# Routing stage of an expert layer: which engine subtracts the low halves of the weight stream

## The chip, the cores and the metric

The kernel runs on one core of one Trainium2 chip. The metric is the device time of one execution in microseconds (us). In the kernel before, three executions took 1796.3 us in the median (1794.24 to 1799.25).

Five engines work side by side, each through its own list of instructions in order: TensorE (PE, matrix products; PEld is its weight load), VectorE (DVE), ScalarE (ACT), GpSimd (POOL), and SyncE (SP), which here only issues loads. An instruction waits until the semaphores that it names have been raised by other engines or by DMAs.

## What is computed

Two transformer blocks in a row, on 256 positions of width 1024. The change lies in the last layer of the second block, a product-key layer with 16384 one-neuron experts. Cut to that layer, the reference is:

```
q = (x @ wq).reshape(B, L, 8, 2, 128)
s = jnp.einsum('blhpd,hpkd->blhpk', q, keys)            # 128 keys in each of 16 lists
ts, ti = lax.top_k(s, 16)                               # 16 best of each list
cand = ts[..., 0, :, None] + ts[..., 1, None, :]        # 16 x 16 sums for each head
cs, ci = lax.top_k(cand.reshape(B, L, 8, 256), 16)
e1 = take_along_axis(ti[..., 0, :], ci // 16, axis=-1)
e2 = take_along_axis(ti[..., 1, :], ci % 16, axis=-1)
g = softmax(cs)
act = gelu(x_t . u_tab[e]) * g                          # for each of the 8 x 16 chosen experts
out = sum of act * v_tab[e]
```

The kernel computes the product of x with the whole of `u_tab` (128 blocks of 128 experts), spreads the chosen weights into a dense matrix, and multiplies with the whole of `v_tab`. So which experts are chosen is needed only when the dense matrix is built.

## The kernel before

**The weight stream.** All weights come as 544 blocks of 128 x 1024 in the order of use. SP loads each block into one of three `raw` buffers. Products are computed from rounded operands in three matmuls each, so each block is split: ACT copies `raw` to a rounded high half `wh` (line 250), and the low half `wl` is `raw` minus `wh` (line 252), made by VectorE or by GpSimd. There are four buffers each of `wh` and `wl`. `Stream.next()` hands out block i and first writes the split of block i + 3 into the instruction lists. A `raw` buffer can be loaded again once its low half is made. The rule for the engine is one attribute, `pool_every`: 0 gives every low half to VectorE, 1 every one to GpSimd, and 2 those of even number.

**The products.** `gemm_w` takes one block as eight groups of three matmuls: high half by the high x (line 304), high half by the low x (305), low half by the high x (306).

**The queries.** Sixteen blocks of `wq` give sixteen query tiles `qb` (line 1437). For each, two steps later, four short matmuls with `keys` (1421), and one step after that two searches `top16` on VectorE (lines 1411 to 1415), each of five operations over 128 scores: eight largest, their positions, replacement, again eight largest and positions.

**The routes.** Beside the first blocks of `u_tab` (`experts_in`: two blocks, one gelu on ACT at line 1396, one store of the result) runs the generator `route`, once for each half of the positions. Each block is followed by one step of it. The 18 steps of one route are: one with the cast `vf` and the 128 x 2048 sum `cand`; eight with a search of 256 candidates each; one with the softmax (`ex`, an Exp on ACT at line 1460, `pos`, `ee`); six wide ones of 128 x 2048 elements that look the indices up (twice a comparison at 1475, a product at 1478, a reduction at 1480); one empty one; one with three transposes on PE (1485), which read the reductions' result; and one with their copy `eT`, in which the next route begins. The two routes go with 20 pairs of blocks. After them, with `pool_every` at 0, the remaining 88 blocks of `u_tab` go side by side with the dense matrix, most of whose work is VectorE's (lines 1518 to 1539).

**What sets the order.** Every engine's list is written out by the program's order; nothing is rearranged afterwards. A low half that VectorE makes stands in its list between the pieces of searches and routes; one that GpSimd makes stands in a list that holds nothing else in this stage.

Of the kernel before, what the change touches and what calls it, by code (L numbers as in the profile page):

```python
# [283 lines left out]
def body(ctx, tc, a, o, upto=99):  # L284
# [4 lines left out]
    ws = Stream(nc, P0, [a["ws"], a["us"], a["vs"]])  # L289
    pump = Pump()  # L290

    def psum(tag):
        return PS.tile([128, 512], F32, tag=tag, name=tag, bufs={"mm": 2, "acc": 3, "od": 1, "tr": 2}[tag])
# [14 lines left out]
    def gemm_w(out, w, xs, nk=8, base=0):  # L308
        h, lo = w
        for n in range(nk):  # L310
            sl = slice((base + n) * 128, (base + n + 1) * 128)
            mm3(out, h[:, sl], lo[:, sl], xs[0][n], xs[1][n], n == 0, n == nk - 1)

    def gemm_pair(outs, xs, shared=False):

        ws_ = [ws.next(), ws.next(AHEAD - 1)]
        for low in range(2):
            for n, k in enumerate(KORD):
                sl = slice(k * 128, k * 128 + 128)
                for i in range(2):  # L320
                    h, lo = ws_[i]
                    if low:
                        nc.tensor.matmul(outs[i], lo[:, sl], xs[0][k], start=False,
                                         stop=n == 7 and not (shared and i == 0))
                    else:
                        nc.tensor.matmul(outs[i], h[:, sl], xs[0][k], start=n == 0 and not (shared and i), stop=False)
                        nc.tensor.matmul(outs[i], h[:, sl], xs[1][k], start=False, stop=False)
# [1061 lines left out]
    def experts_in(i, between=pump.step):  # L1389
        pt = psum("mm")  # L1390
        gemm_w(pt[:, :T], ws.next(), xs_x)
        between()
        gemm_w(pt[:, T:], ws.next(), xs_x)
        st = PP.tile([128, 2, T], F32, tag="st", name="st", bufs=2)
        last[i] = st
        nc.scalar.activation(st, pt.rearrange("p (e t) -> p e t", e=2), AF.Gelu_apprx_tanh)  # L1396
        if i < 62:
            nc.scalar.dma_start(stored[i // 4][:, 2 * (i % 4):2 * (i % 4) + 2, :], st)
# [3 lines left out]
    with tc.tile_pool(name="route", bufs=1) as RP:  # L1402
        keys = RP.tile([128, 16, 128], F32, name="keys")
        nc.gpsimd.dma_start(keys, a["keys"])
        nc.gpsimd.dma_start(iota, a["iota"])
        v = RP.tile([128, 2, 16, 16], F32, name="v")
        vi = RP.tile([128, 2, 16, 16], U32, name="vi")

        def top16(val, idx, src, n):
            scr = RP.tile([128, 256], F32, tag="scr", name="scr", bufs=1)  # L1410
            nc.vector.max(val[:, 0:8], src)
            nc.vector.max_index(idx[:, 0:8], val[:, 0:8], src)
            nc.vector.match_replace(scr[:, :n], val[:, 0:8], src, -3.0e38)
            nc.vector.max(val[:, 8:16], scr[:, :n])
            nc.vector.max_index(idx[:, 8:16], val[:, 8:16], scr[:, :n])

        def key_scores(b, qb):
            yield
            pt = psum("acc")
            for tt in range(2):  # L1420
                nc.tensor.matmul(pt[:, tt * 128:tt * 128 + 128], qb[:, tt * 128:tt * 128 + 128], keys[:, b, :],
                                 start=True, stop=True)
            yield
            for tt in range(2):
                top16(v[:, tt, b], vi[:, tt, b], pt[:, tt * 128:tt * 128 + 128], 128)

        first = [psum("mm"), psum("mm")]
        gemm_pair([pt[:, :T] for pt in first], xs_x)
        for b in range(16):
            if b < 2:  # L1430
                pt = first[b]
            else:
                pt = psum("mm")
                ws.pool_every = 2
                gemm_w(pt[:, :T], ws.next(), xs_x)
            qb = RP.tile([128, T], F32, tag="qb", name="qb", bufs=3)
            nc.scalar.copy(qb, pt[:, :T])
            pump.step()
            pump.add(key_scores(b, qb))

        def route(tt):
            B4 = [128, 8, 16, 16]
            vf = RP.tile([128, 16, 16], F32, tag="vf", name="vf", bufs=1)
            nc.vector.tensor_copy(vf, vi[:, tt])
            cand = RP.tile([128, 8, 256], F32, tag="cand", name="cand")
            vv = v[:, tt].rearrange("p (h two) k -> p h two k", two=2)
            fv = vf.rearrange("p (h two) k -> p h two k", two=2)
            nc.vector.tensor_tensor(cand.rearrange("p h (i j) -> p h i j", i=16),
                                    vv[:, :, 0, :, None].to_broadcast(B4),
                                    vv[:, :, 1, None, :].to_broadcast(B4), op=ALU.add)  # L1450
            cs = RP.tile([128, 8, 16], F32, tag="cs", name="cs", bufs=1)
            ci = RP.tile([128, 8, 16], U32, tag="ci", name="ci", bufs=1)
            yield
            for h in range(8):
                top16(cs[:, h], ci[:, h], cand[:, h], 256)
                yield
            ee = RP.tile([128, 3, 8, 16], F32, tag="ee", name="ee", bufs=1)
            ex = RP.tile([128, 8, 16], F32, tag="ex", name="ex", bufs=1)
            nc.vector.tensor_tensor(ex, cs, cs[:, :, 0:1].to_broadcast([128, 8, 16]), op=ALU.subtract)
            nc.scalar.activation(ex, ex, AF.Exp)  # L1460
            pos = RP.tile([128, 2, 8, 16], F32, tag="pos", name="pos", bufs=1)
            cf = RP.tile([128, 8, 16], F32, tag="cf", name="cf", bufs=1)
            nc.vector.tensor_copy(cf, ci)
            nc.vector.tensor_scalar(pos[:, 0], cf, 1.0 / 16.0, -7.5 / 16.0, op0=ALU.mult, op1=ALU.add)
            nc.vector.tensor_scalar(pos[:, 0], pos[:, 0], MAGIC, None, op0=ALU.add)
            nc.vector.tensor_scalar(pos[:, 0], pos[:, 0], -MAGIC, None, op0=ALU.add)
            nc.vector.scalar_tensor_tensor(pos[:, 1], pos[:, 0], -16.0, cf, op0=ALU.mult, op1=ALU.add)
            sm = RP.tile([128, 8], F32, tag="sm", name="sm", bufs=1)
            nc.vector.tensor_reduce(sm, ex, axis=AX.X, op=ALU.add)
            nc.vector.reciprocal(sm, sm)  # L1470
            nc.vector.tensor_tensor(ee[:, 2], ex, sm[:, :, None].to_broadcast([128, 8, 16]), op=ALU.mult)
            yield
            for p in range(2):
                oh = RP.tile([128, 8, 16, 16], F32, tag="oh", name="oh")
                nc.vector.tensor_tensor(oh, pos[:, p, :, :, None].to_broadcast(B4),
                                        iota[:, None, None, :16].to_broadcast(B4), op=ALU.is_equal)
                yield
                nc.vector.tensor_tensor(oh, oh, fv[:, :, p, None, :].to_broadcast(B4), op=ALU.mult)
                yield
                nc.vector.tensor_reduce(ee[:, p], oh, axis=AX.X, op=ALU.add)  # L1480
                yield
            yield
            pt = psum("tr")
            for n in range(3):
                nc.tensor.transpose(pt[:, n * 128:n * 128 + 128], ee[:, n].rearrange("p h k -> p (h k)"), ident)
            yield
            nc.scalar.copy(eT[tt], pt[:, :384].rearrange("p (n t) -> p n t", n=3))

        def route_all():
            yield  # L1490
            yield
            for tt in range(2):
                yield from route(tt)

        pump.add(route_all())
        while pump.active:
            experts_in(n_in[0])
            n_in[0] += 1
            pump.step()
        ws.pool_every = 0  # L1500
# [135 lines left out]
```

## Time and profile before

| what | before |
|---|---|
| median of three executions | 1796.3 us |
| the profiled execution | 1792.96 us |
| its span, first to last instruction | 1791.1 us |
| PE busy, share of the span | 97% |
| DVE busy | 74% |
| ACT busy | 52% |
| POOL busy | 18% |
| mean granted clock of TensorE | 0.991 |
| granted clock, 950 to 1146 us | 0.97 |

The queries begin at about 950 us of the span, the first block of `u_tab` at about 1000, the first matmuls of the dense matrix at 1146.5. A busy share is a mean over stages with different limits; what matters for this change is what PE waits for between 950 and 1146. In a row of the timeline the first number is the start, the second the duration, both in us; a bracket at the end gives how long the engine had been idle before it and what ended that. PEclk is the granted clock of TensorE as a share of full speed: 1.00 is 2.4 GHz, 0.50 is 1.2 GHz.

### The profile page before, as it was taken

The numbers are of one execution on the slowest core, as the hardware profiler recorded it, in microseconds if no ns is written. First come the engines' busy times: TensorE is split into PE (matmuls) and PEld (weight loads), VectorE is DVE, ScalarE is ACT, GpSimd is POOL, SyncE is SP. The second block draws the span as 40 slices with busy tenths as digits, with TensorE's granted clock in tenths as the row PEclk, the third lists the DMA queues.
The fourth block names the chain that finished last, engine by engine and source line by source line (L and its number), as shares of the span: only waits on it lengthen the run. The fifth ranks groups of instructions, "written<-read, shape, count | busy, mean of one in ns | idle before, by whom it ended". The sixth has DMA issues, their size and how long they took to land.

```text
span 1791.1 us, 30504 instructions
## 1 busy us (share of the span) xinstructions
PE 1729.7 (97%) x11790; PEld 1581.5 (88%) x11794; DVE 1332.6 (74%) x2177; ACT 936.1 (52%) x1515; POOL 319.1 (18%) x249
## 2 busy tenths in 40 slices
PE   8999999999999999999899889899999999999998
PEld 7999888999899987997799889899999988888886
DVE  5665668855665645888767999899999977776766
ACT  5544556545464435685545345455555545545554
POOL 3000133221300101000003344100000033333332
PEclk9999999999999999999999999999999999999999
DMA  7656453444476653553255456566665677777775
GB/s 235 191 174 196 148 164 106 138 134 156 162 216 190 198 166 117 167 188 106 91 180 191 140 189 219 199 195 190 200 198 191 199 249 252 243 241 240 244 239 173
DMA packets 93410, 332.08 MB, mean 185 GB/s; under 512 B 10552, under 2 KB 10707, under 8 KB 90960
## 3 DMA queue, kind: packets, MB, share of 16 engines
q1 hardware_dynamic: 79488, 287.73, 50.0%
q0 software_dynamic: 3696, 21.67, 3.6%
q10 hardware_dynamic: 10080, 20.71, 3.2%
q8 instruction: 93, 1.52, 0.4%
q14 instruction: 53, 0.43, 0.1%
HBM read 311.73 MB, written 18.35 MB: 184 GB/s over the span
## 4 chain that ended last, share of the span: by engine, by line
PE 62%; DVE 26%; issue 4%; ACT 4%; DMA 3%; POOL 1%; ACTq 0%; POOLq 0%; SPq 0%; DVEq 0%
PE mm L304 10%; PE mm L306 9%; PE mm L305 9%; PE acc L306 7%; PE acc L305 7%; PE acc L304 7%; DVE wl L252 7%; DVE oh L1523 5%; DVE gd L1539 2%; PE od L304 2%; PE od L305 2%; PE od L306 2%; DVE oh L1518 2%; ACT wh L250 2%; DMA raw<-in_us_dram 1%
## 5 line engine op out<-in xcount | busy, mean ns | idle before, releaser
L252 DVE TENSOR_TENSOR wl<-raw,wh 128x1024 fp32r<-128x1024 f32 x502 | 651.9, 1302 | 281.7 <-ACT wh L250 279.6
L306 PE MATMUL mm<-hT,wl 128*128 128x256 f32 (+1 forms) x2496 | 706.5, 283 | 10.7 <-DVE wl L252 10.7
L304 PE MATMUL mm<-hT,wh 128*128 128x256 f32 (+1 forms) x2496 | 715.0, 286 | 1.7 <-ACT rxp L1227 1.3
L250 ACT CAST wh<-raw 128x1024 fp32r<-128x1024 f32 x544 | 570.4, 1052 | 262.1 <-DMA raw<-in_us_dram 73.2
L305 PE MATMUL mm<-lT,wh 128*128 128x256 f32 (+1 forms) x2496 | 706.3, 283 | 0.0
L306 PEld LDWEIGHTS mm<-hT,wl 128*128 128x128 f32 x2496 | 475.5, 191 | 11.7 <-DVE wl L252 11.7
L304 PEld LDWEIGHTS mm<-hT,wh 128*128 128x128 f32 x2496 | 475.1, 190 | 10.4 <-issue 5.5
L305 PEld LDWEIGHTS mm<-lT,wh 128*128 128x128 f32 x2496 | 473.9, 190 | 3.4 <-issue 1.4
L306 PE MATMUL acc<-wh,al 128*128 128x512 f32 x516 | 202.1, 392 | 0.5 <-DVE al L344 0.5
L304 PE MATMUL acc<-wh,ah 128*128 128x512 f32 x516 | 202.0, 391 | 0.0
L305 PE MATMUL acc<-wl,ah 128*128 128x512 f32 x516 | 201.5, 391 | 0.1
L252 POOL TENSOR_TENSOR wl<-raw,wh 128x1024 fp32r<-128x1024 f32 x42 | 111.1, 2646 | 198.0 <-ACT wh L250 198.0
L1523 DVE SCALAR_TENSOR_TENSOR oh<-iota,eT,wp 128x256 fp32r<-128x256 f32 x256 | 117.3, 491 | 0.0
L306 PEld LDWEIGHTS acc<-wh,al 128*128 128x128 f32 x516 | 96.8, 188 | 21.8 <-DVE al L344 1.1
L305 PEld LDWEIGHTS acc<-wl,ah 128*128 128x128 f32 x516 | 96.9, 188 | 20.2 <-DVE wl L252 0.5
L304 PEld LDWEIGHTS acc<-wh,ah 128*128 128x128 f32 x516 | 96.9, 188 | 19.2 <-issue 0.3
L343 ACT CAST ah<-sv 128x256 fp32r<-128x256 f32 x124 | 50.5, 407 | 120.6 <-PE od L305 44.8
L344 DVE TENSOR_TENSOR al<-sv,ah 128x256 fp32r<-128x256 f32 x124 | 77.5, 625 | 39.0 <-ACT ah L343 38.8
L1564 POOL TENSOR_TENSOR sv<-sv,gd 128x512 f32<-128x512 f32 x62 | 101.3, 1660 | 5.7 <-DMA sv<-act 5.3
L1396 ACT ACTIVATE st<-mm 128x512 f32<-128x512 f32 x64 | 38.3, 598 | 75.9 <-PE mm L306 75.8
L1538 ACT COPY gd<-acc 128x256 f32<-128x256 f32 x128 | 46.5, 402 | 59.3 <-PE acc L1533 42.9
L417 POOL TENSOR_SCALAR ssq<-ssq 128x1 f32<-128x1 f32 x18 | 8.1, 450 | 356.4 <-ACT junk L415 327.6
(388 smaller groups left out, 2198.5 us busy)
## 6 DMA issues: line engine op xcount, KB each, us to landing
raw<-in_ws_dram SPq DMA_DIRECT2D x288, 512.0 KB, 3.8
raw<-in_us_dram SPq DMA_DIRECT2D x128, 512.0 KB, 3.6
raw<-in_vs_dram SPq DMA_DIRECT2D x128, 512.0 KB, 4.3
act<-st ACTq DMA_DIRECT2D x62, 256.0 KB, 2.7
sv<-act POOLq DMA_DIRECT2D x15, 1024.0 KB, 7.7
gate_w<-in_gate_w_dram ACTq DMA_DIRECT2D x2, 1024.0 KB, 5.6
gain<-in_gains_dram POOLq DMA_DIRECT2D x3, 512.0 KB, 6.7
res<-x SPq DMA_DIRECT2D x2, 512.0 KB, 4.2
```

Source lines behind the costliest of these rows:

```text
L250: nc.scalar.copy(h, raw)
L252: eng.tensor_tensor(lo, raw, h.bitcast(F32), op=ALU.subtract)
L304: nc.tensor.matmul(out, lh, rh, start=start, stop=False)
L305: nc.tensor.matmul(out, lh, rl, start=False, stop=False)
L306: nc.tensor.matmul(out, ll, rh, start=False, stop=stop)
L343: nc.scalar.copy(h, src)
L344: (eng or nc.vector).tensor_tensor(lo, src, h.bitcast(F32), op=ALU.subtract)
L1396: nc.scalar.activation(st, pt.rearrange("p (e t) -> p e t", e=2), AF.Gelu_apprx_tanh)
L1518: nc.vector.tensor_tensor(o1, iota[:, None, :].to_broadcast([128, ONE, 128]), eT[tt][:, 0, tl:tl + ONE, None].to_broadcast([128, ONE, 128] ...
L1523: nc.vector.scalar_tensor_tensor(oh, iota[:, None, :].to_broadcast([128, 2, 128]), eT[tt][:, 1, tl:tl + 1], wp[:, :, tl:tl + 1].bitcast(F3 ...
L1538: nc.scalar.copy(g, v[:, 1])
L1564: nc.gpsimd.tensor_tensor(src, src, gd[:, e:e + 2, :], op=ALU.mult)
```

## The change

Four assignments of `pool_every`. In the queries, from the third block on, it becomes 1 instead of 2. In a route it becomes 0 before `cand`, 1 before the eight searches, and 0 again before the softmax. The old value held from the queries to the end of the routes.

```
@@ queries
                 pt = psum("mm")
-                ws.pool_every = 2
+                ws.pool_every = 1
                 gemm_w(pt[:, :T], ws.next(), xs_x)
@@ route
             nc.vector.tensor_copy(vf, vi[:, tt])
+            ws.pool_every = 0
             cand = RP.tile([128, 8, 256], F32, tag="cand", name="cand")
...
             yield
+            ws.pool_every = 1
             for h in range(8):
                 top16(cs[:, h], ci[:, h], cand[:, h], 256)
                 yield
+            ws.pool_every = 0
             ee = RP.tile([128, 3, 8, 16], F32, tag="ee", name="ee", bufs=1)
```

Lines behind line 1445 have numbers higher by one to three in the changed kernel.

GpSimd's list, from the load of `keys` (with it the queries begin) to the first operation of the dense stage. Before:

```order
L420 TENSOR_TENSOR rstd<-ssq_9919 128x1
L421 TENSOR_TENSOR rstd<-rstd,nhalf 128x1
L1404 DMA keys<-in_keys_dram 128x2048
L1405 DMA iota<-in_iota_dram 128x128
L252 TENSOR_TENSOR wl<-raw,wh 128x1024 x28
L1564 TENSOR_TENSOR st<-st,gd 128x512
```

And in the changed kernel:

```order
L420 TENSOR_TENSOR rstd<-ssq_9919 128x1
L421 TENSOR_TENSOR rstd<-rstd,nhalf 128x1
L1404 DMA keys<-in_keys_dram 128x2048
L1405 DMA iota<-in_iota_dram 128x128
L252 TENSOR_TENSOR wl<-raw,wh 128x1024 x34
L1567 TENSOR_TENSOR st<-st,gd 128x512
```

GpSimd has 34 low halves in a row instead of 28, and they lie elsewhere: 18 are split in the queries and the first three steps after them, 8 in the searches of each route.

VectorE's list in the searches of a route, as one piece of the difference (`cs` and `ci` are values and positions of the best sums, `scr` is what the search leaves over):

```order
 L1414 MAX cs<-scr 128x8
 L1415 MAX_INDEX ci<-cs,scr 128x8
-L252 TENSOR_TENSOR wl<-raw,wh 128x1024
 L1411 MAX cs<-cand 128x8
 L1412 MAX_INDEX ci<-cs,cand 128x8
```

The low half that stood after every second search is gone; the same goes for the searches of the queries.

VectorE's list behind the softmax of the first route (`oh` is the wide tile, `ee` the result). Before:

```order
L1471 TENSOR_TENSOR ee<-ex,sm 128x128
L252 TENSOR_TENSOR wl<-raw,wh 128x1024
L1475 TENSOR_TENSOR oh<-pos,iota 128x2048
L1478 TENSOR_TENSOR oh<-oh,vf 128x2048
L252 TENSOR_TENSOR wl<-raw,wh 128x1024
L1480 TENSOR_REDUCE ee<-oh 128x128
L1475 TENSOR_TENSOR oh<-pos,iota 128x2048
L252 TENSOR_TENSOR wl<-raw,wh 128x1024
L1478 TENSOR_TENSOR oh<-oh,vf 128x2048
L1480 TENSOR_REDUCE ee<-oh 128x128
```

And in the changed kernel:

```order
L1474 TENSOR_TENSOR ee<-ex,sm 128x128
L252 TENSOR_TENSOR wl<-raw,wh 128x1024
L1478 TENSOR_TENSOR oh<-pos,iota 128x2048
L252 TENSOR_TENSOR wl<-raw,wh 128x1024
L1481 TENSOR_TENSOR oh<-oh,vf 128x2048
L252 TENSOR_TENSOR wl<-raw,wh 128x1024
L1483 TENSOR_REDUCE ee<-oh 128x128
L252 TENSOR_TENSOR wl<-raw,wh 128x1024
L1478 TENSOR_TENSOR oh<-pos,iota 128x2048
L252 TENSOR_TENSOR wl<-raw,wh 128x1024
L1481 TENSOR_TENSOR oh<-oh,vf 128x2048
L252 TENSOR_TENSOR wl<-raw,wh 128x1024
```

Here VectorE has a low half ahead of each of the six wide operations, where it had three in all, and GpSimd makes none.

## Rows read from the trace of the kernel before

**Rows 1.** What PE waited for, 950 to 1146: total us, times, longest.

```profile
PE mm L306 <- DVE wl L252: 10.7, 5, 4.1
PE tr L1485 <- DVE ee L1480: 5.0, 2, 3.7
PE acc L1421 <- DVE scr L1413: 2.3, 2, 1.4
```

**Rows 2.** Stretches: length, busy of PE, PEld, DVE, ACT, POOL, then PEclk.

```profile
1020.00:1026.00 6.00, 5.70 (x35) 5.71 (x36) 5.76 (x20) 1.74 (x3) 1.07 (x1) 0.72 0.50 175
1062.00:1070.00 8.00, 6.61 (x35) 6.61 (x36) 7.97 (x5) 2.10 (x3) 2.07 (x2) 0.57 0.37 135
1132.00:1138.00 6.00, 4.90 (x29) 4.90 (x30) 4.23 (x3) 2.97 (x4) 2.93 (x1) 0.72 0.33 111
1072.00:1080.00 8.00, 6.71 (x58) 6.47 (x57) 6.87 (x4) 2.97 (x4) 3.13 (x1) 1.00 0.47 164
```

**Rows 3.** Timeline of POOL and DVE, wide operations of the first route.

```profile
1052.95 2.62 POOL L252 TENSOR_TENSOR wl<-raw,wh 128x1024 fp32r<-128x1024 f32 x1 [3.21 <-ACT wh L250]
1058.05 4.21 POOL L252 TENSOR_TENSOR wl<-raw,wh 128x1024 fp32r<-128x1024 f32 x1 [2.48 <-ACT wh L250]
...
1053.23 4.49 DVE L1475 TENSOR_TENSOR oh<-pos,iota 128x2048 f32<-128x2048 f32 x1
```

**Rows 4.** Line 1412: ns min/median/max, first and last start; POOL timeline in the queries.

```profile
L1412 DVE FIND_INDEX8 vi<-v,acc x32: 288/291/294, 958.7 to 1022.1; 128x8 uint32<-128x128 f32 x32
...
L1412 DVE FIND_INDEX8 ci<-cs,cand x16: 418/419/421, 1026.4 to 1104.7; 128x8 uint32<-128x256 f32 x16
...
964.75 2.40 POOL L252 TENSOR_TENSOR wl<-raw,wh 128x1024 fp32r<-128x1024 f32 x1 [4.08 <-ACT wh L250]
```

**Rows 5.** Timeline of ACT: copies that wait for PE, two queries, two gelus.

```profile
966.64 0.38 ACT L1437 COPY qb<-mm 128x256 f32<-128x256 f32 x1 [1.97 <-PE mm L306]
...
969.92 0.38 ACT L1437 COPY qb<-mm 128x256 f32<-128x256 f32 x1 [1.97 <-PE mm L306]
...
1087.61 0.60 ACT L1396 ACTIVATE st<-mm 128x512 f32<-128x512 f32 x1 [0.69 <-PE mm L306]
...
1098.97 0.60 ACT L1396 ACTIVATE st<-mm 128x512 f32<-128x512 f32 x1 [0.45 <-PE mm L306]
```

**Rows 6.** Timeline of DVE: two low halves, two searches of 256 between them.

```profile
1091.87 1.21 DVE L252 TENSOR_TENSOR wl<-raw,wh 128x1024 fp32r<-128x1024 f32 x1
...
1097.48 1.21 DVE L252 TENSOR_TENSOR wl<-raw,wh 128x1024 fp32r<-128x1024 f32 x1
```

**Rows 7.** Chain that ended last, 1068 to 1143: start, us, what.

```profile
1068.18 3.09 POOL wl L252
1071.29 3.48 DMA raw<-in_us_dram
...
1075.99 3.14 POOL wl L252
...
1136.86 5.94 DMA raw<-in_us_dram
```

**Rows 8.** Timeline of ACT: table load ahead of the softmax's Exp.

```profile
1047.39 1.28 ACT L1460 ACT_TABLE_LOAD   x1 [0.39 <-ACT st L1396]
```

**Rows 9.** Timeline of DVE: wide operations of the first route, with a low half.

```profile
1063.26 2.27 DVE L1480 TENSOR_REDUCE ee<-oh 128x128 f32<-128x2048 f32 x1
1065.57 2.29 DVE L1475 TENSOR_TENSOR oh<-pos,iota 128x2048 f32<-128x2048 f32 x1
1067.78 1.22 DVE L252 TENSOR_TENSOR wl<-raw,wh 128x1024 fp32r<-128x1024 f32 x1
1068.91 4.50 DVE L1478 TENSOR_TENSOR oh<-oh,vf 128x2048 f32<-128x2048 f32 x1
```

**Rows 10.** Stretches behind the routes, columns as in rows 2.

```profile
1138.00:1144.00 6.00, 6.00 (x53) 6.00 (x53) 0.03 (x1) 2.66 (x4) 2.39 (x1) 1.00 0.76 288
1145.00:1300.00 155.00, 151.72 (x1249) 148.64 (x1249) 154.99 (x297) 82.46 (x141) 0.00 (x0) 1.00 0.61 199
```

More of the change, by code (lines that the diff above doesn't have):

```diff
@@ L1433, in body @@
                 pt = psum("mm")
-                ws.pool_every = 2
+                ws.pool_every = 1
                 gemm_w(pt[:, :T], ws.next(), xs_x)
@@ L1444, in route @@
             nc.vector.tensor_copy(vf, vi[:, tt])
+            ws.pool_every = 0
             cand = RP.tile([128, 8, 256], F32, tag="cand", name="cand")
@@ L1453, in route @@
             yield
+            ws.pool_every = 1
             for h in range(8):
@@ L1456, in route @@
                 yield
+            ws.pool_every = 0
             ee = RP.tile([128, 3, 8, 16], F32, tag="ee", name="ee", bufs=1)
```

## The prediction

> **What bounds the kernel now.** I read the waits of PE first, between 950 and 1146 us, the only stretch in which the change moves anything. PE waited there 10.7 us for low halves of VectorE, 5.0 us at the transposes for the reductions, and 2.3 us for a search to give back a score buffer: 18.0 us, and every releaser is VectorE [rows 1]. Next come the stretches with their granted clock. Behind three of these waits TensorE ran at the lower level (1.2 GHz) for some microseconds: the mean is 0.72 over 6 us, 0.57 over 8 us and 0.72 over 6 us, which loses 1.7, 3.4 and 1.7 us of full speed [rows 2]. In the second, PE still stood idle for about a microsecond, which would be counted twice, so I take 6.5 us together. Waits and slow clock make 24.5 us, and no version that leaves PE its work can gain much more here.
>
> Why is VectorE late? The timelines of VectorE and GpSimd give two causes. It has low halves to make between its searches, and its operations with two tensor inputs and GpSimd's low halves exclude each other: a comparison that began 0.28 us behind a GpSimd low half took 4.49 us, the rest of that low half's 2.62 us and then about its own 2.2; and the low half at 1058.05, which met the next product, took 4.21 us instead of 2.40 [rows 3, 4].
>
> PE's pace: a query costs 969.92 - 966.64 = 3.28 us with its score matmuls [rows 5]; two gelus that waited for PE are two pairs apart, so a block of `u_tab` costs (1098.97 - 1087.61) / 4 = 2.84 us [rows 5].
>
> **The change part by part.**
>
> *Low halves in the queries and searches go to GpSimd (34 instead of 28).* On VectorE a low half occupies 1.13 us up to the next start [rows 9]. Two searches of 256 with one low half take 5.61 us [rows 6], so one search takes (5.61 - 1.13) / 2 = 2.24. Beside a block of 2.84 us that leaves VectorE 0.6 us in each step, where the old mean of 2.81 left nothing. In the queries a search covers half as many scores; by its position search, 0.29 against 0.42 us, it lasts some 2.24 x 0.29 / 0.42 = 1.55 us (an estimate), two of them 3.1 per query. With a low half at every second query that was 3.1 + 0.56 = 3.7 us, over PE's 3.28, which explains the 2.3 us of waits [rows 1, 4]; without it VectorE is under PE's pace. So the waits for score buffers and for low halves in these phases should go.
>
> GpSimd must then sustain one low half per block: 2.40 us against 3.28 or 2.84. The 2.40 was taken between searches, and the position searches vary by no more than 6 ns around 0.29 us and 3 ns around 0.42, with GpSimd making low halves beside many of them [rows 4]. So a search and a low half do not hold each other up. The Trainium skill (Perfetto Trace Analysis, Optimizing Scalar/DVE Operations) warns that moving work between VectorE and GpSimd might not help, because they share a read port. Rows 3 agree for operations with two inputs, rows 4 don't for searches; the rule taken without that difference gives the last rival.
>
> The `raw` buffer is now held for 2.40 us by GpSimd at every block. One turn of a buffer, low half to low half, took 1075.99 - 1068.18 = 7.81 us with a low half of 3.09 [rows 7]; with 2.40 it is 7.12, and with three buffers 2.37 us per block, under 2.84. That stays hidden while a load takes less than 3.48 + 3 x (2.84 - 2.37) = 4.9 us.
>
> At the start of the queries GpSimd gets its first three low halves close together, where VectorE made the second before. It is then behind by about one low half, with blocks needed three paces after they are split; I cost that at nothing, at most one low half, 2.4 us.
>
> *No low half on GpSimd during the wide operations.* VectorE now makes ten per route around them. A comparison or product occupies 2.21 us, a reduction 2.31, a low half 1.13 [rows 9]: 3.34, 3.34 and 3.44 us per step, 2 x 10.12 = 20.24 for the six, against 6 x 2.84 = 17.0 on PE. So VectorE falls behind by 3.2 us in each route whatever happens, but without the 2.2 us that four wide operations and several low halves lost to GpSimd. Call X the time at which PE ends the block to which the softmax step belongs (a gelu starts there). VectorE reaches the first of these low halves at X + 3.6: gelu 0.60 [rows 5], 0.39 to the table load and 1.28 for it [rows 8] make 2.27; the Exp and the last small operations of the softmax, or ACT's next copy, take 1.3 more (an estimate from the few tenths that such rows last). The last reduction ends at X + 3.6 + 20.2 = X + 23.8. PE reaches the transposes after eight more blocks, X + 22.7. It waits about 1.2 us, in each route: 2.4 us together, where it waited 5.0 [rows 1]. The clock stayed at 1.00 around the old wait of this kind in the first route, which was 5.0 - 3.7 = 1.3 us [rows 1, 2], so I charge no slow clock; were it to fall, 1.7 us each.
>
> The low halves themselves stay in time: the split runs three blocks ahead, 8.5 us, and the last one among the wide operations ends at X + 25.0, with its block beginning at X + 27.2 (eight blocks, the wait and the transposes, and one more). Margins before it are at least 1.4 us. At the two changes of `pool_every` a late GpSimd low half can hold `cand` or a small softmax operation: between 0 and 2.4 us on VectorE, four times, which the 0.6 us saved in each of eight searches cover; on PE I take nothing.
>
> *Behind the routes.* VectorE bounds the dense stage, busy 154.99 of 155 us; but before that it stands idle (0.03 of 6 us busy) [rows 10]. So it carries no debt into the dense stage, the stage begins earlier by what PE gained, and lasts as long as before. ACT's, SP's and GpSimd's lists keep their order; only who raises a `raw` buffer's release changes.
>
> *Sum.* 24.5 us of waits and slow clock, less 2.4 that remain at the transposes: 22.1 us. The span goes from 1791.1 to 1769.0 us, the profiled execution from 1792.96 to 1770.9. The median of the runs shown is 3.3 us above the profiled execution, so I forecast **1774 us**.
>
> **The rivals.**
>
> *Loads bind the search phases.* If loads slow down beside the stores of results, as the one of 5.94 us [rows 7], a turn is 7.12 + 5.94 - 3.48 = 9.58 us, 3.19 per block. Some 17 of the 34 low halves are paced by 2.84: 17 x 0.35 = 6 us are given back, 1780 us. Against it: the turn in rows 7 had a load of 3.48, and it decides only from 4.9 us.
>
> *VectorE is late at both transposes.* If the wide steps or the softmax take longer than I put them, PE waits 3.7 us twice, as it did once, each followed by a slow clock of 1.7: 10.8 instead of 2.4 us remain, 1782 us.
>
> *The change doesn't do what it says, or the gain is lost again.* The wide operations could still meet GpSimd's low halves at the edges, or the dense stage could start no earlier, being held by loads: 1796 us. Against it: the list of GpSimd is empty for ten blocks per route, and VectorE is idle ahead of the dense stage [rows 10].
>
> *Slower: GpSimd becomes the bound.* If searches and low halves do hold each other up, a low half takes up to 4.21 us, the longest one in rows 3, at every block: 17 x (4.21 - 3.28) + 17 x (4.21 - 2.84) = 39 us of new waits, and the 2.4, against 24.5 removed: 17 us slower, 1813 us. It decides from a low half of (22.1 + 17 x 6.12) / 34 = 3.7 us. Rows 4 speak against it.
>
> **How the numbers follow.** The forecast gets 0.70, loads 0.12, late transposes 0.08, no effect 0.05, slower 0.05. The first three are faster by more than 0.3% (5 us, about what a measurement of this kernel can tell from no change): 0.90; 0.05 within it; 0.05 slower. The range reaches down to all 24.5 us and the 2 us by which the fastest run lies below the median, with some room for small losses not listed (1768), and up to the two middle rivals with the 2.4 us of the slow start and one run's spread (1786).
>
> **What would show it.** In the profile of the changed kernel PE's waits for `wl` and for the score buffers are near zero; those at the transposes are about 1.2 us twice; the granted clock is 1.00 throughout; every wide operation takes 2.3 us; the low halves on GpSimd take 2.4 us, those on VectorE 1.2; the first matmul of the dense matrix comes about 22 us earlier, and the dense stage is as long as before. I am wrong if low halves on GpSimd are over 3 us beside searches, if PE waits for a low half that waited for ACT or a load, or if the dense stage gets longer by what the routes got shorter.

## The result

The changed kernel takes 1771.5 us in the median of four executions (1769.41 to 1777.5), against 1795.3 us of the kernel before on the same chip (1792.21 to 1799.25): a ratio of 0.9878, with a 95% interval of 0.9864 to 0.9892. A second session gave 1771.5 against 1794.2 us, 0.9873 (0.9858 to 0.9889). The forecast was 1774 us, in a range of 1768 to 1786.

The profiled execution of the changed kernel is the longest of the four (1777.5 us; span 1775.7). A profile of the second session has a span of 1768.3 us. Of the 7.4 us between the two, 5.4 lie behind the dense stage and 1.2 ahead of the stretch that the change moves; that stretch itself takes 170.0 us in the one and 169.2 in the other, so it is read from the first.

### The profile page after: what moved, and what is told of

Same layout as the page of the kernel before. It is cut to its first block, busy times and chain, and to the rows that moved or that the text cites. A ratio compares the mean times of both kernels' runs of the same rounds, so it can differ in the third digit from the quotient of the medians.

```text
span 1775.7 us, 30510 instructions
## 1 busy us (share of the span) xinstructions
PE 1723.6 (97%) x11790; PEld 1574.3 (89%) x11794; DVE 1321.8 (74%) x2171; ACT 934.0 (53%) x1515; POOL 307.3 (17%) x255
## 4 chain that ended last, share of the span: by engine, by line
PE 68%; DVE 21%; issue 4%; ACT 3%; DMA 2%; POOL 1%; ACTq 0%; POOLq 0%; SPq 0%; DVEq 0%
PE mm L304 12%; PE mm L306 12%; PE mm L305 12%; PE acc L306 7%; PE acc L305 7%; PE acc L304 6%; DVE wl L252 6%; DVE oh L1526 5%; DVE gd L1542 2%; DVE oh L1521 2%; PE od L304 2%; PE od L305 2%; PE od L306 2%; ACT wh L250 1%; DMA raw<-in_vs_dram 1%
## 5 line engine op out<-in xcount | busy, mean ns | idle before, releaser
L252 POOL TENSOR_TENSOR wl<-raw,wh 128x1024 fp32r<-128x1024 f32 x48 | 114.9, 2403 | 139.9 <-ACT wh L250 97.2
L1526 DVE SCALAR_TENSOR_TENSOR oh<-iota,eT,wp 128x256 fp32r<-128x256 f32 x256 | 113.5, 468 | 0.0
L1567 POOL TENSOR_TENSOR sv<-sv,gd 128x512 f32<-128x512 f32 x62 | 85.3, 1406 | 6.0 <-DMA sv<-act 5.7
L344 DVE TENSOR_TENSOR al<-sv,ah 128x256 fp32r<-128x256 f32 x124 | 68.6, 553 | 19.8 <-ACT ah L343 19.3
```

The costliest lines, as they stand in the source:

```text
L252: eng.tensor_tensor(lo, raw, h.bitcast(F32), op=ALU.subtract)
L344: (eng or nc.vector).tensor_tensor(lo, src, h.bitcast(F32), op=ALU.subtract)
L1526: nc.vector.scalar_tensor_tensor(oh, iota[:, None, :].to_broadcast([128, 2, 128]), eT[tt][:, 1, tl:tl + 1], wp[:, :, tl:tl + 1].bitcast(F3 ...
L1567: nc.gpsimd.tensor_tensor(src, src, gd[:, e:e + 2, :], op=ALU.mult)
```

## The profile after, read against the rows of before

What PE waited for in the queries and routes, in the form of rows 1 (total us, times, longest); the last line stands at the start of the queries in both kernels:

```profile
PE tr L1488 <- DVE ee L1483: 1.8, 2, 0.9
PE acc L1536 <- DVE oh L1526: 0.7, 1, 0.7
PE mm L304 <- ACT qb L1437: 0.4, 1, 0.4
```

The 10.7 us for low halves and the 2.3 us for score buffers of rows 1 are gone. Of the 5.0 us at the transposes 1.8 are left. The 0.7 us belong to the first step of the dense stage.

The stretch from the queries to the end of the routes, columns as in rows 2: first the kernel before, then the changed kernel, then its dense stage, which answers to rows 10.

```profile
950.00:1146.00 196.00, 177.63 (x1440) 175.53 (x1439) 176.23 (x452) 82.97 (x104) 77.51 (x28) 0.97 0.54 185
...
950.00:1124.00 174.00, 171.06 (x1443) 170.07 (x1442) 156.90 (x448) 83.84 (x105) 81.35 (x34) 1.00 0.65 210
...
1124.00:1279.00 155.00, 151.87 (x1255) 149.18 (x1254) 154.99 (x296) 82.16 (x141) 0.00 (x0) 1.00 0.61 198
```

PE runs the same matmuls (1440 and 1443 records) in 22 us less, and its clock is granted in full, where rows 2 had three stretches at the lower level. Of the 22 us, 177.6 - 171.1 = 6.6 are busy time of PE, and the other 15.4 are time in which it stood idle. VectorE is busy 176.2 - 156.9 = 19 us less: it makes six low halves fewer, some 7 us (an estimate: six of 1.2), and most of the rest is time in which an instruction only stood waiting for GpSimd.

How long that stretch is, from PE's first matmul of the third query to the first matmul of the dense matrix (the latter from the line's statistics: min/median/max ns, first and last start). Before, then after:

```profile
953.61 0.38 PE L304 MATMUL mm<-hT,wh 128*128 128x256 f32 x1 [0.39 <-ACT qb L1437]
...
L1533 PE MATMUL acc<-oh,oh x256: 277/282/389, 1146.5 to 1422.0; 128*128 128x256 f32 x128
```

```profile
953.29 0.38 PE L304 MATMUL mm<-hT,wh 128*128 128x256 f32 x1 [0.39 <-ACT qb L1437]
...
L1536 PE MATMUL acc<-oh,oh x256: 278/282/387, 1123.3 to 1398.8; 128*128 128x256 f32 x128
```

192.9 us became 170.0: 22.9 us. The dense stage then lasts 275.5 us in both, from its first matmul's start to its last's. So what was won in the routes was kept whole through the dense stage.

VectorE's timeline at the wide operations of the first route, which answers to rows 3 and 9:

```profile
1038.11 1.23 DVE L252 TENSOR_TENSOR wl<-raw,wh 128x1024 fp32r<-128x1024 f32 x1
1039.25 2.28 DVE L1478 TENSOR_TENSOR oh<-pos,iota 128x2048 f32<-128x2048 f32 x1
1041.45 1.22 DVE L252 TENSOR_TENSOR wl<-raw,wh 128x1024 fp32r<-128x1024 f32 x1
1042.59 2.28 DVE L1481 TENSOR_TENSOR oh<-oh,vf 128x2048 f32<-128x2048 f32 x1
...
1055.93 2.27 DVE L1483 TENSOR_REDUCE ee<-oh 128x128 f32<-128x2048 f32 x1
```

No wide operation of 4.5 us is left; a step is 3.34 us long. And GpSimd beside the searches, which answers to rows 4 (all 34 low halves, then the position searches of both sizes, then two low halves back to back):

```profile
L252 POOL TENSOR_TENSOR wl<-raw,wh x34: 2385/2401/2482, 954.5 to 1086.7; 128x1024 fp32r<-128x1024 f32 x34
...
L1412 DVE FIND_INDEX8 vi<-v,acc x32: 287/290/292, 957.3 to 1008.1; 128x8 uint32<-128x128 f32 x32
L1412 DVE FIND_INDEX8 ci<-cs,cand x16: 418/419/421, 1014.2 to 1082.7; 128x8 uint32<-128x256 f32 x16
...
1014.01 4.75 POOL L252 TENSOR_TENSOR wl<-raw,wh 128x1024 fp32r<-128x1024 f32 x2 [3.73 <-ACT wh L250]
```

Both are as long as they were when GpSimd made half as many there.

## The experiments

Three theories were put to the runs. A: VectorE is late because of the low halves in its own list and because its two-input operations and GpSimd's low halves exclude each other, and lateness is carried from one stage to the next. B: only the number of low halves on VectorE counts. C: only the exclusion counts. The first four runs share a chip and 14 executions of the kernel before (median 1793.6 us), the others a chip and 16 executions (1794.2).

### Only the queries

```
# kernel before, with
-                ws.pool_every = 2
+                ws.pool_every = 1
...
+        ws.pool_every = 2
         def route(tt):
```

> Only the queries give every low half to GpSimd; the routes keep every second one, wide operations included. Theory A (VectorE is late by its own low halves and by its two-input operations excluding GpSimd's, and lateness is carried from stage to stage): the waits for score buffers (2.3 us), the first low-half waits of the routes (2.3, 1.6 and 1.0 us) and one stretch of slow clock (1.7) go, and the wide operations start with less lateness: 9 to 16 us faster than before, about 1783 us. Rival B (only the number of low halves on VectorE counts): VectorE has about as few as in the changed kernel, so the whole gain, about 1772. Rival C (only the exclusion counts): only a few collisions in the queries go, 1790 or more.

1785.0 us, ratio 0.9953 (0.9936 to 0.9969). PE's waits:

```profile
PE mm L306 <- DVE wl L252: 7.1, 3, 3.8
PE tr L1487 <- DVE ee L1482: 4.7, 2, 3.7
```

The waits for score buffers are gone and low-half waits are down from five to three; those at the wide operations stay (3.8 and 2.4 us, where the kernel before had 4.1 and 1.7). GpSimd has 35 low halves from 950 to 1150, one more than in the changed kernel (34), and yet 13 us of the gain are missing. B falls; A had 1783.

### Only the routes

The changed kernel with `pool_every = 2` in the queries.

> Only the routes switch (none on GpSimd around the wide operations, all in the searches); the queries keep every second one. Theory A: the score-buffer waits and the first waits behind them stay (6 to 8 us with the slow clock), the rest goes: about 1779 us. Rival B: VectorE has more low halves than before (GpSimd 25 instead of 28), so no gain, 1795 to 1799. Rival C: nearly the whole gain, 1775 or less.

1784.6 us, 0.9955 (0.9939 to 0.997): faster, so B is wrong here too, but A was 6 us too hopeful. PE's waits, then the piece of VectorE's timeline where the longest arose:

```profile
PE mm L306 <- DVE wl L252: 6.4, 2, 5.8
PE acc L1421 <- DVE scr L1413: 2.3, 2, 1.4
PE tr L1488 <- DVE ee L1483: 1.9, 2, 0.9
...
1020.70 2.29 DVE L1449 TENSOR_TENSOR cand<-v 128x2048 f32<-128x2048 f32 x1
1022.90 3.37 DVE L252 TENSOR_TENSOR wl<-raw,wh 128x1024 fp32r<-128x1024 f32 x1
```

VectorE comes to `cand` at 1020.7; in the changed kernel it is there at 1010.4. The low half behind `cand` is VectorE's in this kernel, since `pool_every` is 0 there, and PE waits 5.8 us for it. The kernel before had three waits around this place, 2.3, 1.6 and 1.0 us. Where VectorE is late, the zero ahead of `cand` costs; in the changed kernel it doesn't, because the queries leave no lateness. The two parts gave 8.6 and 9.0 us alone, 22.7 together. The 5 us that the sum of the parts lacks are hardly clear of the noise, since each of the three gains is known to about 3 us; in the profiled executions the stretch gets shorter by 8.0, 12.3 and 22.9 us, where only 2.6 are lacking.

### Every low half on GpSimd

The kernel before with 1 in place of 2.

> GpSimd makes every low half from the third query to the end of the routes, none is left to VectorE. Theory A: at the wide operations a comparison or product and a low half take turns, 2.2 + 2.4 = 4.6 us a step against 2.84 on PE, so PE waits some 3 us more per route than in the changed kernel, with slow clock behind it: about 1781 us. Rival B: VectorE has the least to do, 1771 or less. Rival C: wide operations at 4.5 us throughout, no better than before, 1793 or more.

1783.6 us, 0.9947 (0.9931 to 0.9964), near A's 1781, and neither B's 1771 nor C's 1793. PE's waits, then VectorE's timeline and the row of GpSimd that goes with it:

```profile
PE mm L306 <- POOL wl L252: 7.6, 8, 1.3
...
1038.13 2.29 DVE L1475 TENSOR_TENSOR oh<-pos,iota 128x2048 f32<-128x2048 f32 x1
1040.45 4.38 DVE L1478 TENSOR_TENSOR oh<-oh,vf 128x2048 f32<-128x2048 f32 x1
1044.86 2.29 DVE L1480 TENSOR_REDUCE ee<-oh 128x128 f32<-128x2048 f32 x1
1047.18 4.40 DVE L1475 TENSOR_TENSOR oh<-pos,iota 128x2048 f32<-128x2048 f32 x1
...
1038.34 29.03 POOL L252 TENSOR_TENSOR wl<-raw,wh 128x1024 fp32r<-128x1024 f32 x8 [2.30 <-ACT wh L250]
```

Comparisons and products take turns with low halves: 4.4 us, and 29.03 / 8 = 3.6 us for a low half. The reduction takes its 2.29 us although GpSimd has a low half to make throughout. So the exclusion goes with the operation's form, and it is GpSimd that PE waits for here, not VectorE. A's waits came, 7.6 us over both routes where it had some 6. The slow clock that A set behind them did not: the granted clock is 1.00 from 950 to 1150.

### Every low half on VectorE

The kernel before with 0 in place of 2.

> VectorE makes every low half of the queries and the routes, GpSimd none. Theory A: no exclusion, but 3.1 + 1.1 = 4.2 us per query against 3.28 on PE (15 us over 16 queries) and 3.4 per search step against 2.84; with the 3 us per route at the wide operations that is 25 to 30 us late, about where the kernel before is: 1790 to 1800 us. Rival B: 28 more low halves of 1.13 us on VectorE, 1815 or more. Rival C: with the exclusion gone the whole gain, 1772.

1795.8 us, 1.0013 (1.0004 to 1.0023): a little slower than before, and within A's 1790 to 1800. There is no exclusion in this kernel, and nothing is won by that: C falls. There are 28 more low halves on VectorE, and little is lost: B falls. PE's waits:

```profile
PE mm L306 <- DVE wl L252: 8.3, 17, 3.6
PE acc L1421 <- DVE scr L1413: 5.8, 8, 0.8
PE tr L1485 <- DVE ee L1480: 5.1, 2, 2.6
```

The score matmuls that wait for VectorE come every 4.30 us, where A had 4.2 us per query.

### Only the wide operations

The changed kernel with 2 in place of 1 in the queries and in the searches.

> Queries and searches keep every second low half on GpSimd as before; only around the wide operations VectorE makes all. It separates the exclusion from the lateness that the queries and searches build up. Theory A: wide operations at 2.3 us, but VectorE enters them as late as before, with 3 more low halves a route: the 2.3 us at the score buffers and some 6 to 8 us of low-half waits with slow clock stay, 1782 to 1790 us. Rival C (only the exclusion counts): close to the changed kernel, 1774 or less. Rival B (only the number of low halves on VectorE): it has more than before, no gain, 1794 or more.

1786.5 us, 0.9954 (0.994 to 0.9968), within A's 1782 to 1790. PE's waits:

```profile
PE mm L306 <- DVE wl L252: 6.5, 2, 5.8
PE tr L1488 <- DVE ee L1483: 3.5, 2, 2.6
PE acc L1421 <- DVE scr L1413: 2.2, 2, 1.3
```

The wait of 5.8 us behind `cand` is here too. Taking the exclusion away around the wide operations gives some 8 us of the 22.7. Giving GpSimd the searches too adds nothing that can be told from noise in a kernel whose queries are late (1784.6 against 1786.5, on two chips and inside each other's spread).

### GpSimd's low halves made longer

```
             eng.tensor_tensor(lo, raw, h.bitcast(F32), op=ALU.subtract)
+            if self.longer and eng is nc.gpsimd:
+                eng.tensor_tensor(lo[:, :512], raw[:, :512], h[:, :512].bitcast(F32), op=ALU.subtract)
```

`longer` is set from the third query to the end of the routes of the changed kernel; half of each low half is made twice.

> The changed kernel, in which GpSimd, in the queries and routes, makes half of each low half a second time, so that one takes about 3.6 us instead of 2.4. This prices the rival in which GpSimd becomes the bound. By the prediction's price (every microsecond over PE's pace is a wait): 17 x (3.6 - 3.28) + 17 x (3.6 - 2.84) = 18 us are given back, about 1790 us. Other theory: the three blocks of lead and GpSimd's rest around the wide operations absorb most of it, since 8 searches run up only 6 us of lateness: 2 to 8 us given back, 1774 to 1780 us.

1794.5 us, 1.0003 (0.9993 to 1.0013): the time before, to what can be measured. PE's waits for GpSimd, then GpSimd's timeline (a low half and its half again, then the next), and two of these waits in PE's timeline:

```profile
PE mm L309 <- POOL wl L255: 11.8, 19, 2.6
...
984.12 2.40 POOL L253 TENSOR_TENSOR wl<-raw,wh 128x1024 fp32r<-128x1024 f32 x1
986.60 1.28 POOL L255 TENSOR_TENSOR wl<-raw,wh 128x512 fp32r<-128x512 f32 x1
987.84 2.40 POOL L253 TENSOR_TENSOR wl<-raw,wh 128x1024 fp32r<-128x1024 f32 x1
...
987.94 0.39 PE L309 MATMUL mm<-hT,wl 128*128 128x256 f32 x1 [0.17 <-POOL wl L255]
991.65 0.39 PE L309 MATMUL mm<-hT,wl 128*128 128x256 f32 x1 [0.17 <-POOL wl L255]
```

A low half now takes 3.7 us from start to start, and PE steps at that pace: 991.65 - 987.94 = 3.71. The prediction's rival had put the point at which the change turns from faster to slower at 3.7 us per low half; this run stands on that point. The theory that the three blocks of lead would absorb most of it is wrong: GpSimd needs 3.71 us per block where PE needs 3.28 in the queries and 2.84 in the searches, so it falls behind from the first query on. That the total comes out at the turning point is in part luck, though, because two things that the price leaves out offset each other. The lead did absorb the first lateness: PE's weight load first waits for a low half at 976.8, the sixth one, after some 2.5 us (an estimate: 6 x 0.43). Against that PE waits 4.2 us at the transposes instead of 1.8, and the mean granted clock is 0.95 over two stretches of 35 us (1005 to 1040 and 1065 to 1100), some 3.5 us. The run also shows how much longer a low half of the changed kernel can get before the whole gain is gone, 1.3 us.

### A later load in the last stage

```
-            if e % 8 == 7 and e < 120:
-                fetch(e // 8 + 2)
+            if e % 8 == 3 and 8 <= e < 120:
+                fetch(e // 8 + 1)
```

> The changed kernel with another edit in the last stage: the load that GpSimd issues for the stored activations stands four blocks later in its list, which breaks its four multiplications in a row into two and two. If the 5 to 9 us that VectorE's low halves took in that stage come from GpSimd's uninterrupted row of multiplications, the longest are about 3.6 us, the last stage loses its few waits, and the time is 0 to 4 us below the changed kernel's. If they come from something else, both stay as they were.

> The changed kernel once more, beside the run with the later load: 1771 us, and 22 us under the kernel before.

1774.0 us (0.9889; 0.9871 to 0.9907) with the later load, 1771.5 us (0.9873; 0.9858 to 0.9889) without it: no gain. VectorE's low halves in the last stage (ns min/median/max), with the later load and without:

```profile
L252 DVE TENSOR_TENSOR wl<-raw,wh x130: 1209/1224/3831, 1398.8 to 1754.5; 128x1024 fp32r<-128x1024 f32 x130
```

```profile
L252 DVE TENSOR_TENSOR wl<-raw,wh x130: 1209/1225/6504, 1396.9 to 1749.6; 128x1024 fp32r<-128x1024 f32 x130
```

The cause was named rightly (the longest falls from 6.5 to 3.8 us as the row of multiplications is broken), but PE waits little for these operations: 0.9 us for VectorE in the whole stage without the later load, 2.5 with it, one profiled execution each. In the longest execution of the changed kernel it was 4.4.

## Why the prediction was right, step by step

**Waits and slow clock, 24.5 us.** Right, in its two terms too. The stretch lost 22.9 us and the forecast for it was 22.1: 15.6 of waits (18.0 less the 2.4 that should remain), where 15.4 of idle time went, and 6.5 of slow clock, where 6.6 of busy time went. The granted clock is 1.00 throughout, so the slow clock went with the waits, as the sum had it.

**Low halves to GpSimd in queries and searches.** Right. A search and a low half don't hold each other up, and 2.40 us per low half stays under PE's 3.28 and 2.84. At the start of the queries GpSimd has four low halves in a row, not the three of the prediction, and PE doesn't wait for them. The price of the rival was right too, in its sum: at 3.7 us per low half the gain is gone. In the queries of the kernel before the prediction put VectorE's lateness down to the number of its low halves alone, 3.7 us a query. Its low halves do come 7.48 us, two queries, apart from 961.97 to 984.41. From 991.88 on four in a row met a low half of GpSimd's and took 1.95 to 2.96 us, and they come 8.2 to 8.9 us apart. So the exclusion made VectorE late in the queries as well.

**Wide operations.** The softmax step was taken as the start at X + 3.6 us, with X the start of a gelu. In the profile that gelu starts at 1034.55 and VectorE's first low half at 1038.11, X + 3.56. Six steps were to take 20.24 us; the last reduction ends at 1055.93 + 2.27 = 1058.20, X + 23.65 instead of 23.8. PE waits 0.9 us at the transposes of each route instead of 1.2; the prediction's own terms make it 23.8 - 22.7 = 1.1.

**The edges.** The prediction let a GpSimd low half hold a small softmax operation for up to 2.4 us at each change, at no cost. In the first route two low halves in a row held two operations, about 4.0 us together (`ex` takes 0.27 us unheld, the cast 0.22). It cost PE nothing, because the sum of the softmax has to wait for ACT's Exp anyway, but it was close: VectorE's last small operation before that sum ended at 1037.05, the Exp at 1037.14. That part came out with some luck. GpSimd's, VectorE's and ACT's timelines in the first route:

```profile
1031.05 4.80 POOL L252 TENSOR_TENSOR wl<-raw,wh 128x1024 fp32r<-128x1024 f32 x2 [0.92 <-ACT wh L250]
...
1031.58 2.02 DVE L1462 TENSOR_TENSOR ex<-cs 128x128 f32<-128x128 f32 x1
1033.53 2.42 DVE L1466 CAST cf<-ci 128x128 f32<-128x128 uint32 x1
...
1036.83 0.31 ACT L1463 ACTIVATE ex<-ex 128x128 f32<-128x128 f32 x1
...
1037.17 0.29 DVE L1472 TENSOR_REDUCE sm<-ex 128x8 f32<-128x128 f32 x1
```

**Behind the routes.** Right: the dense stage is as long as before and begins 23 us earlier.

**The rivals.** PE waits for no low half between 950 and 1124, so loads didn't bind the search phases, and GpSimd didn't become the bound. The transposes cost 0.9 us twice, not 3.7.

**The 2.5 us between 1774 and 1771.5.** Some 0.8 us are the stretch (22.9 instead of 22.1). Another 1.0 to 2.1 are the median of before, from which the forecast subtracts: 1796.3 us in the three runs shown, 1795.3 and 1794.2 in the two series beside the changed kernel. What separates the rest is not settled.

**What the prediction did not price** is the parts by themselves. The runs with one part show 8.6 and 9.0 us, 17.6 together, which is less than the 22.7 of the whole, though hardly by more than the noise. One reason shows in the run with only the routes: the lateness that the queries left there became a wait of 5.8 us behind `cand`.

## What to carry to other kernels

When an engine that is late feeds another in list order, count its load stage by stage against the pace of the engine that it feeds, and follow the lateness through to the next stage: a part of such a change can be worth less alone, where lateness that another part would have removed turns up as a wait further on. When work is shared out between VectorE and GpSimd, go by the form of what VectorE does at that moment: in this kernel searches and reductions went on beside GpSimd's low halves, two-input operations and some small one-input ones were held by them. Give a rival its turning point in a measured unit (here 3.7 us per low half); it can then be tried in one run.

## What the runs showed that was not expected

Operations with one input can be held by GpSimd as well. The cast of 128 x 128 indices above took 2.42 us and ended with the low half beside it; in the second route it took 0.21; there a scalar operation of the same size took 2.30 us, 0.23 otherwise, beside a low half that ended at about the same time:

```profile
1086.70 2.48 POOL L252 TENSOR_TENSOR wl<-raw,wh 128x1024 fp32r<-128x1024 f32 x1 [0.58 <-ACT wh L250]
...
1086.19 0.21 DVE L1466 CAST cf<-ci 128x128 f32<-128x128 uint32 x1
...
1086.96 2.30 DVE L1469 TENSOR_SCALAR pos<-pos 128x128 f32<-128x128 f32 x1
```

The Trainium skill (SBUF — State Buffer, Who interferes with whom) says that a VectorE operation with two SBUF inputs contends with a GpSimd operation that reads SBUF, and that casts and scalar operations can enter modes that take both of VectorE's ports and then contend too. These durations agree with that, but no row shows the mode.

Multiplications that stand in GpSimd's list without a wait between them can hold VectorE for all of them, not for one. Near the end of the longest execution six took 7.50 us, a low half of VectorE beside them 8.75, and PE waited 2.60 us for it. At the same place of the second session's profile, whose two rows stand last, six took 10.35 us, and two low halves of VectorE got in between, 2.31 us each:

```profile
1724.75 7.50 POOL L1567 TENSOR_TENSOR sv<-sv,gd 128x512 f32<-128x512 f32 x6
...
1724.59 8.75 DVE L252 TENSOR_TENSOR wl<-raw,wh 128x1024 fp32r<-128x1024 f32 x1 [0.98 <-ACT wh L250]
...
1733.39 0.80 PE L305 MATMUL acc<-wl,ah 128*128 128x512 f32 x1 [2.60 <-DVE wl L252]
...
1720.31 10.35 POOL L1567 TENSOR_TENSOR sv<-sv,gd 128x512 f32<-128x512 f32 x6
...
1723.53 2.31 DVE L252 TENSOR_TENSOR wl<-raw,wh 128x1024 fp32r<-128x1024 f32 x1
```

GpSimd's low halves, in the run with all of them there, also let VectorE in after each one (4.4 us per product, not 29), although between 1036 and 1070 only the first of ten waited for ACT. What decides whether VectorE gets in between is open.
